# Loads of the experts' rows for the first two token tiles: from one issuing queue to three

## The chip, the cores and the metric

The kernel runs on one core of one Trainium2 chip. A core has engines that work side by side, each on its own instruction stream: TensorE (PE, with its weight loads shown as PEld), VectorE (DVE), ScalarE (ACT), GpSimd (POOL) and SyncE (SP). SP, ACT and POOL can also issue transfers (DMAs) between device memory and the on-chip memory; 16 DMA engines carry them. The metric is device time in microseconds (us), the median of three executions.

## The reference

Two decoder layers over 512 tokens of width 1024. What matters here is the second half of a layer: a mixture of 16 experts, of which every token takes two, and a gated residual behind it.

```python
y = jnp.zeros(x.shape, jnp.float32)
for e in range(N_EXPERTS):
    hdn = jax.nn.silu(x @ w_gate[e]) * (x @ w_up[e])
    y = y + combine[..., e:e + 1] * (hdn @ w_down[e])       # combine: two weights a token
...
h = h + hier_moe(rmsnorm(h, ffn_norm[i]), ...)
gate = jax.nn.sigmoid(rmsnorm(h, ple_norm[i]) @ ple_gate_w[i] + ple_gate_b[i])
h = h + gate * (p[i] @ ple_proj[i])
```

## The kernel before

The 512 tokens are four tiles `h[0]` to `h[3]` of 128 tokens by 1024 columns, kept in on-chip memory. For every expert the kernel gathers up to 128 tokens' rows, multiplies them, and POOL scatters the resulting rows (`ys`) to a table `yd` in device memory (line 1203). The table has 2 x 512 rows: for each token one row from its first expert (k = 0) and one from its second (k = 1).

A loop for overflowing experts follows (`overflow`, line 1251), whose count is a value computed on the chip. Here it runs no pass, but every engine goes through its entry and its end, and there waits until the others have come to it and the scatters have landed.

Then comes `combine`. For tile i and expert rank k it loads 128 rows of `yd` into a tile `yt[i, k]` (line 1363): tile 0 in two column halves of 512 (256 KB each), the other tiles whole (512 KB each). That makes ten loads a layer, in the order of tiles. The words `COMB` (lines 63 to 68), one string for each layer, give the order of the steps behind it. Each step puts its instructions at the end of its engines' streams, so no engine runs ahead of that order in its own stream:

- `p3`: three pieces of the embedding's projection (PE line 1347, copied out by ACT line 1348).
- `c000`, `c010`, `c011`, `c001`: add a half of `yt` times the token's weight to `h[0]` (DVE line 1372). The digits are tile, rank k, half; `c10`, `c11` and so on add a whole tile.
- `t00`, `t01`: PE transposes a half of `h[0]` (line 251); ACT makes its rounded high part `n3h` (line 221), and DVE the low part `n3l` (line 222). `t1` to `t3` do both halves of a tile.
- `g00` and so on: the gate's matmuls (lines 255 to 257, three for each product); `n0` and so on: the squared sum and the reciprocal root of a row's norm (ACT line 210, POOL lines 204 and 205).

The first layer begins `p3 c000 c010 t00 c011 c001 p2 n0 p1 t01 c11 c10 g00 t1`, the second `p3 c000 c010 t00 c001 c011 p1 p2 c11 t01 n0 c10 p3 p9 n1 c20`.

Between the loop and `c000` one more piece of the gate's weights is prepared: ACT makes two 128x512 high parts `wh` (line 232), DVE two low parts `wl` (line 243). They stand ahead of `c000` in DVE's stream. Behind the ten loads SP's stream has the rest of the gate's weights (`wr<-wpg`, line 114) and the next layer's first ones (`wr<-win`).

Of the kernel before, what the change touches and what calls it, by code (L numbers as in the profile page):

```python
# [23 lines left out]
S = 512  # L24
# [143 lines left out]
class _Kernel:  # L168
# [1160 lines left out]
    def combine(self):  # L1329
        nc, V, T, SC, w, h, l, tk = self.nc, self.V, self.T, self.SC, self.w, self.h, self.l, self.ticks  # L1330
# [25 lines left out]
        yt = {}  # L1356
# [3 lines left out]
        for i in range(NT):  # L1360
            for ns in (slice(0, 512), slice(512, D)) if not i else (slice(0, D),):
                for k in range(2):
                    nc.sync.dma_start(yt[i, k][:, ns], self.yd[k * S + i * 128:k * S + (i + 1) * 128, ns])
        w.limit = 10 ** 9
        rn, xn, n3, o, gt, ss = {}, {}, {}, {}, {}, {}

# [210 lines left out]
```

## Time and profile before

| | |
|---|---|
| median of three runs | 925.35 us (923.51 to 927.01) |
| the profiled execution | 925.41 us, its span 923.6 us |
| granted TensorE clock, mean | 0.973 |
| busy share of the span | PE 93%, DVE 77%, ACT 56%, POOL 16% |
| the ten loads of a layer, issued by SP | first layer 399.50 to 406.85 us, second 852.08 to 857.63 us |

A time in a row counts from the start of the span. PE is nearly always busy, so a change in these stretches counts as far as it moves PE's next work: between the loop and the gate's first matmul PE has idle gaps, and each is put down to what ended it. "issue" means that the engine waited for nothing that the profile shows, which here is the way out of the loop.

### The profile page before, as it was taken

To read this page: it belongs to the slowest core of one execution; us is meant where nothing else is said; L and a number is where in the kernel's file an instruction comes from. 1 tells how busy PE (TensorE), PEld (TensorE's weight loads), DVE (VectorE), ACT (ScalarE), POOL (GpSimd) and SP (SyncE) were. 2 spreads that over 40 slices of the span, in tenths; PEclk is the share of its full clock that TensorE was granted. 3 is DMA by queue.
4 is the path that set the end of the run, shared out by engine and by line. 5 is a ranking of instruction groups with operands and counts; after the bars stand their busy time and mean duration, and the time that the engine had idled before them with its cause. 6 is when DMAs were issued, how large, how long until landed. Compare 5 with 4: busy or idle time off the path is not lost. (4 is left out here: it accounts for less than half of the span.)

```text
span 923.6 us, 12348 instructions
## 1 busy us (share of the span) xinstructions
PE 858.0 (93%) x4393; PEld 687.6 (74%) x4393; DVE 715.4 (77%) x1182; ACT 519.1 (56%) x945; POOL 151.2 (16%) x214
## 2 busy tenths in 40 slices
PE   7999988897999999979979999989979999998994
PEld 5888876685677777767878887767847777776783
DVE  4599989966788888746676998998478888885674
ACT  4322246853687878745433233487347778776453
POOL 2040001122222211101010300022131222111101
PEclk9999999998999999999999999989979999999998
DMA  9222230158799979563322223110958998882602
GB/s 354 106 92 96 98 114 1 46 193 309 270 347 363 370 271 340 227 234 146 114 92 92 92 103 112 49 46 24 373 216 307 359 370 324 317 321 91 260 24 91
DMA packets 35775, 179.02 MB, mean 194 GB/s; under 512 B 8064, under 2 KB 8320, under 8 KB 18944
## 3 DMA queue, kind: packets, MB, share of 16 engines
q1 hardware_dynamic: 23472, 148.49, 43.1%
q0 software_dynamic: 9792, 20.99, 6.2%
q10 hardware_dynamic: 2448, 8.73, 2.6%
q8 instruction: 35, 0.57, 0.2%
q14 instruction: 28, 0.23, 0.1%
HBM read 171.89 MB, written 23.07 MB: 211 GB/s over the span
## 5 line engine op out<-in xcount | busy, mean ns | idle before, releaser
L239 DVE TENSOR_TENSOR wl<-wr,wh 128x1024 fp32r<-128x1024 f32 x212 | 253.1, 1220 | 41.4 <-ACT wh L228 40.1
L228 ACT CAST wh<-wr 128x1024 fp32r<-128x1024 f32 x212 | 216.2, 1053 | 91.1 <-PE mm L256 60.9
L255 PE MATMUL mm<-wh,xTh 128*128 128x512 f32 x256 | 113.9, 445 | 1.0 <-ACT xTh L221 1.0
L483 DVE SCALAR_TENSOR_TENSOR acc<-glu,cwh,acc 128x512 f32<-128x512 f32 x120 | 100.5, 837 | 3.4
L257 PE MATMUL mm<-wh,xTl 128*128 128x512 f32 x256 | 101.2, 395 | 1.2 <-DVE xTl L222 1.2
L256 PE MATMUL mm<-wl,xTh 128*128 128x512 f32 x256 | 100.5, 392 | 0.0
L257 PE MATMUL mm<-nhi,wl 128*128 128x512 f32 (+1 forms) x224 | 77.3, 345 | 2.5 <-DVE wl L239 2.5
L255 PE MATMUL mm<-nhi,wh 128*128 128x512 f32 (+1 forms) x224 | 77.1, 344 | 0.0
L256 PE MATMUL mm<-nlo,wh 128*128 128x512 f32 (+1 forms) x224 | 77.0, 344 | 0.0
L255 PEld LDWEIGHTS mm<-wh,xTh 128*128 128x128 f32 x256 | 48.1, 188 | 16.9 <-issue 6.7
L1241 PE MATMUL mm<-wr,hT 128*128 128x512 f32 x128 | 60.2, 592 | 0.0
L1198 POOL DMA_INDIRECT xg<-xnd,ix x32 | 35.4, 1105 | 149.8 <-PE tr L251 136.8
L256 PEld LDWEIGHTS mm<-wl,xTh 128*128 128x128 f32 x256 | 48.2, 188 | 15.3 <-DVE wl L239 6.2
L257 PEld LDWEIGHTS mm<-wh,xTl 128*128 128x128 f32 x256 | 48.0, 188 | 12.9 <-DVE xTl L222 2.9
L255 PE MATMUL mm<-wh,mhi 128*128 128x512 f32 x128 | 54.0, 422 | 1.0 <-DVE h L750 1.0
L1203 POOL DMA_INDIRECT yd<-ys,ix x32 | 32.3, 1010 | 122.9 <-ACT ys L1243 107.3
L255 PE MATMUL mm<-wh,n3h 128*128 128x512 f32 x128 | 50.6, 395 | 0.0
L257 PE MATMUL mm<-wh,mlo 128*128 128x512 f32 x128 | 50.3, 393 | 0.0
L256 PE MATMUL mm<-wl,mhi 128*128 128x512 f32 x128 | 50.0, 391 | 0.0
L257 PE MATMUL mm<-wh,n3l 128*128 128x512 f32 x128 | 49.9, 390 | 0.0
L256 PE MATMUL mm<-wl,n3h 128*128 128x512 f32 x128 | 49.9, 390 | 0.0
L257 PEld LDWEIGHTS mm<-nhi,wl 128*128 128x128 f32 x224 | 42.4, 189 | 8.2 <-DVE wl L239 3.2
(236 smaller groups left out, 1861.6 us busy)
## 6 DMA issues: line engine op xcount, KB each, us to landing
wr<-wgu SPq DMA_DIRECT2D x62, 1024.0 KB, 9.1
wr<-wdn SPq DMA_DIRECT2D x30, 1024.0 KB, 10.8
wr<-win SPq DMA_DIRECT2D x13, 1024.0 KB, 6.2
wr<-wout SPq DMA_DIRECT2D x8, 1024.0 KB, 4.8
wr<-wpg SPq DMA_DIRECT2D x8, 1024.0 KB, 13.8
yt<-yd SPq DMA_DIRECT2D x12, 512.0 KB, 8.1
wr<-wqk SPq DMA_DIRECT2D x4, 1024.0 KB, 4.8
xnd<-xn ACTq DMA_DIRECT2D x8, 512.0 KB, 4.0
```

The costliest lines, as they stand in the source:

```text
L228: self.SC.copy(hi, src)
L239: self.V.tensor_sub(lo, src, h32)
L255: self.T.matmul(o, lh, rh, start=first, stop=False)
L256: self.T.matmul(o, lh, rl, start=False, stop=False)
L257: self.T.matmul(o, ll, rh, start=False, stop=last)
L483: V.scalar_tensor_tensor(acc[:, m], glu[:, m, k:k + S], self.cwh[:, m, k:k + 1], acc[:, m], op0=ALU.mult, op1=ALU.add)
L1198: return self.G.indirect_dma_start(out=dst, out_offset=None, in_=self.xnd[:, :], in_offset=bass.IndirectOffsetOnAxis(ap=col, axis=0), boun ...
L1203: return self.G.indirect_dma_start(out=self.yd[:, :], out_offset=bass.IndirectOffsetOnAxis(ap=col, axis=0), in_=src, in_offset=None, bound ...
L1241: self.T.matmul(o[nh], hT[:, c], wc[:, ns], start=(c == 0), stop=(c == 1))
```

## The change

The loads for rank k = 1 of the first two token tiles are issued by other engines: the two halves of tile 0 (`yt[0, 1]`) by ACT, the whole of tile 1 (`yt[1, 1]`) by POOL. The other loads stay on SP, in the same order. Lines of the changed kernel behind this one have a number higher by one.

```diff
         for i in range(NT):
             for ns in (slice(0, 512), slice(512, D)) if not i else (slice(0, D),):
                 for k in range(2):
-                    nc.sync.dma_start(yt[i, k][:, ns], self.yd[k * S + i * 128:k * S + (i + 1) * 128, ns])
+                    q = (SC, self.G)[i] if k and i < 2 else nc.sync
+                    q.dma_start(yt[i, k][:, ns], self.yd[k * S + i * 128:k * S + (i + 1) * 128, ns])
```

SP's stream in the first layer, behind the loop's end; `yt01` is tile 0 rank 1, `yt11` tile 1 rank 1. Before:

```order
L1363 DMA yt00_4153<-yd0_2304 128x512
L1363 DMA yt01_4154<-yd0_2304 128x512
L1363 DMA yt00_4153<-yd0_2304 128x512
L1363 DMA yt01_4154<-yd0_2304 128x512
L1363 DMA yt10_4155<-yd0_2304 128x1024
L1363 DMA yt11_4156<-yd0_2304 128x1024
L1363 DMA yt20_4157<-yd0_2304 128x1024
```

And now:

```order
L1364 DMA yt00_4153<-yd0_2304 128x512 x2
L1364 DMA yt10_4155<-yd0_2304 128x1024
L1364 DMA yt20_4157<-yd0_2304 128x1024
L1364 DMA yt21_4158<-yd0_2304 128x1024
L1364 DMA yt30_4159<-yd0_2304 128x1024
L1364 DMA yt31_4160<-yd0_2304 128x1024
L114 DMA wr_4171<-wpg 128x2048
```

SP has seven issues where it had ten, and the second half of `yt00` is now its second load. ACT's stream in the first layer, at the same place, the changed kernel against the one before:

```order
 L1251 COMPARE_AND_BRANCH
 L1251 UNCONDITIONAL_BRANCH
+L1364 DMA yt_4154<-yd_2304 128x512 x2
 L232 ACTIVATE wh<-wr,pgain 128x512 x2
 L1348 ACTIVATE pp_3987<-mm 128x256
```

Both issues stand ahead of the two `wh` of the gate's weights. On POOL the load of `yt11` stands between the loop's end and the first norm's `r` (line 204).

## Rows read from the trace of the kernel before

**Rows 1.** Waits, 390 to 430 us: who <- whom: us in total, times, longest.
```profile
POOL r L204 <- DMA yt<-yd: 16.6, 1, 16.6
...
PE tr L251 <- DVE h L1372: 4.5, 3, 1.6
...
DVE h L1372 <- DMA yt<-yd: 1.8, 2, 1.1
```

**Rows 2.** Waits, 845 to 880 us.
```profile
PE tr L251 <- DVE h L1372: 0.3, 1, 0.3
```

**Rows 3.** Timeline of DVE, first layer: start, us, what [idle before <- releaser].
```profile
401.39 1.41 DVE L243 SCALAR_TENSOR_TENSOR wl<-wr,pgain,wh 128x512 fp32r<-128x512 f32 x2 [6.18 <-ACT wh L232]
...
404.23 0.75 DVE L1372 SCALAR_TENSOR_TENSOR h<-yt,wts,h 128x512 f32<-128x512 f32 x1 [0.67 <-DMA yt<-yd]
406.35 0.69 DVE L222 TENSOR_TENSOR n3l<-tr,n3h 128x512 fp32r<-128x512 f32 x1 [1.37 <-ACT n3h L221]
408.16 1.54 DVE L1372 SCALAR_TENSOR_TENSOR h<-yt,wts,h 128x512 f32<-128x512 f32 x2 [1.12 <-DMA yt<-yd]
```

**Rows 4.** Timeline of PE, first layer.
```profile
405.04 0.66 PE L251 MATMUL tr<-con,h 128*128 128x128 f32 x4 [1.46 <-DVE h L1372]
405.53 2.75 PE L1347 MATMUL mm<-wr,pT 128*128 128x256 f32 x12
409.75 0.44 PE L251 MATMUL tr<-con,h 128*128 128x128 f32 x2 [1.47 <-DVE h L1372]
```

**Rows 5.** Timeline of SP, loads one by one: three of the first layer, one of the second.
```profile
399.50 0.33 SPq L1363 DMA_DIRECT2D yt<-yd  x1
...
399.87 1.79 SPq L1363 DMA_DIRECT2D yt<-yd  x1
...
402.38 0.42 SPq L1363 DMA_DIRECT2D yt<-yd  x1
...
852.08 0.33 SPq L1363 DMA_DIRECT2D yt<-yd  x1
```

**Rows 6.** Landing times: loads 2 and 4 (first layer), 2 (second): us from issue.
```profile
yt<-yd SPq DMA_DIRECT2D x1, 256.0 KB, 4.3
...
yt<-yd SPq DMA_DIRECT2D x1, 256.0 KB, 5.7
...
yt<-yd SPq DMA_DIRECT2D x1, 256.0 KB, 3.8
```

**Rows 7.** Stretches, first layer: busy us by engine, PEclk, DMA share, GB/s.
```profile
401.20:402.40 1.20, 1.20 (x7) 1.04 (x7) 1.01 (x2) 1.07 (x3) 0.00 (x0) 1.00 0.25 63
...
408.20:414.00 5.80, 4.33 (x22) 3.60 (x22) 3.76 (x5) 1.90 (x4) 0.76 (x2) 1.00 1.03 420
```

**Rows 8.** Timeline of ACT, its first instructions behind the loop, both layers.
```profile
400.63 1.33 ACT L232 ACTIVATE wh<-wr,pgain 128x512 fp32r<-128x512 f32 x2 [1.65 <-issue]
...
853.20 1.33 ACT L232 ACTIVATE wh<-wr,pgain 128x512 fp32r<-128x512 f32 x2 [1.46 <-issue]
```

**Rows 9.** By tile and line: DMA issues of ACT (gv) and POOL (wgu), ns min/median/max.
```profile
L200 ACTq DMA_DIRECT2D gv<-gv x6: 334/340/378, 121.2 to 882.3; - x6
...
L114 POOL DMA_DIRECT2D wr<-wgu x2: 614/616/617, 233.3 to 685.3; - x2
...
DMA to landing us min/median/max: 5.8/7.0/8.1
```

**Rows 10.** Timeline of DVE and PE, second layer.
```profile
856.31 0.75 DVE L1372 SCALAR_TENSOR_TENSOR h<-yt,wts,h 128x512 f32<-128x512 f32 x1 [0.28 <-DMA yt<-yd]
...
859.54 2.84 DVE L1372 SCALAR_TENSOR_TENSOR h<-yt,wts,h 128x512 f32<-128x512 f32 x3
...
853.30 4.54 PE L1347 MATMUL mm<-wr,pT 128*128 128x256 f32 x12 [1.98 <-issue]
857.68 0.60 PE L251 MATMUL tr<-con,h 128*128 128x128 f32 x4
```

**Rows 11.** Stretches, second layer: the projection's matmuls behind the loop.
```profile
853.44:856.86 3.42, 3.42 (x9) 2.71 (x10) 2.63 (x4) 1.48 (x3) 0.00 (x0) 0.50 1.05 284
```

## The prediction

> **What bounds the kernel now.** I first read the waits of the two stretches that the change touches, since the loads are used only between the overflow loop and the gate. In the first layer DVE's `c` steps wait 1.8 us in two pieces for loads of `yt`, and PE's transposes wait 4.5 us in three pieces for those steps; POOL waits 16.6 us and has nothing else to do [rows 1]. In the second layer PE waits for them once, 0.3 us [rows 2]. So there is some 3 us to win in the first layer at most, and next to nothing in the second.
>
> Then the timelines, in the order of the chain. First layer: SP issues load 2 (`yt01`, half 0) at 399.87 [rows 5]; it lands after 4.3 us [rows 6], at 404.2, and `c010` starts at 404.23 after an idle 0.67 [rows 3]. It ends at 404.98, and `t00` starts at 405.04 [rows 4]. DVE's `n3l` for it ends at 406.35 + 0.69 = 407.04, 2.00 behind the start of `t00`. Then DVE is idle for 1.12 until load 4 (`yt01`, half 1) has landed: issued at 402.38, 5.7 us, so 408.1. `c011` and `c001` take 1.54 from 408.16 to 409.70, and `t01` starts at 409.75. PE had idled 1.47 there; its projections had ended at 405.53 + 2.75 = 408.28 [rows 3 to 6]. Load 4 is late because SP's issue of load 2 took 1.79 where others take 0.33 and 0.42 [rows 5]: from 401.20 to 402.40 the DMA engines were busy for 0.25 of the time, and later, with all loads queued, for all of it at 420 GB/s [rows 7].
>
> Second layer: no such stall. `c010` waits 0.28 for its load, but `t00` starts at 857.68 because PE's twelve projections end there: they take 4.54 [rows 10], at a granted clock of 0.50 from 853.44 to 856.86 [rows 11], against 2.75 for the same twelve in the first layer [rows 4]. `c001`, `c011` and `c11` then run without a gap, 2.84 for the three [rows 10]; their data was there.
>
> **The change part by part.** *Three loads leave SP.* This saves SP three issues of about 0.42 [rows 5]. Nothing waits for SP's later loads in these stretches, so in itself it is worth 0. What can be worth something is the hole of 401.20 to 402.40 [rows 7], which other queues may fill. In the second layer there is no wait of PE that an earlier load could end, so 0 there.
>
> The Trainium skill ("DMA: Bandwidth & Descriptors", Issuing engines are not separate DMA queues) says that DMAs from several engines run on the same 16 DMA engines, and that issuing from several saves only the issuing time. The rows agree where the DMA engines are full, at 420 GB/s, and not in the hole, where the issue itself was what was late. By the rule alone the sum would be the 0 of the paragraph above.
>
> *Two issues enter ACT's stream, ahead of `wh`.* ACT's own issues cost 0.34 each [rows 9], so 0.68; the bounds are 0.66, two of SP's cheapest, and 3.6, two of its 1.79 [rows 5]. I take 0.68, from ACT's rows. First layer: `wl` ends at 401.39 + 1.41 + 0.68 = 403.48, `c000` 0.75 later, and `c010` could start at 404.23, just when it does now: its old wait of 0.67 hides the two issues. Without that cover they would cost 0.68. Second layer: `c010` could start at 856.31 - 0.28 + 0.68 = 856.71 [rows 10]; it needs to end by about 857.62 for `t00` at 857.68, so to start by 856.87. Hidden, with 0.16 to spare.
>
> *`yt01` is issued later, by ACT.* ACT does its first work behind the loop at 400.63 and 853.20 [rows 8], SP at 399.50 and 852.08 [rows 5]: ACT is out 1.1 us later, and that is 0.76 behind load 2's old issue in the first layer (399.87) and about 0.7 in the second (856.31 less 3.8 is 852.5). When it lands is the unknown. The nearest rows are the same load's 4.3 (first layer) and 3.8 (second); the upper end is load 4's 5.7 [rows 6]; the lower end is that it is no longer late at all. In the first layer I take 4.3: landed at 404.93, `c010` 0.70 later than now, `t00` at 405.74, its `n3l` done at 407.74. Half 1, issued at 400.97 with 4.3 to 5.7, lands at 405.3 to 406.7, and `yt00`'s half 1, now SP's second load, at 399.87 + 4.3 = 404.2 or 405.6 with 5.7. Both are there before 407.74, so DVE's wait of 1.12 is gone: 407.74 + 1.54 + 0.05 puts `t01` at 409.33, not 409.75. Gain 0.42. The ends: with no load late, `t00` stays at 405.04 and `t01` comes at 405.04 + 2.00 + 1.54 + 0.05 = 408.63, a gain of 1.12 (PE is free at 408.28). With 5.7 `c010` starts at 406.33, 2.10 late, and `t01` at 410.73, a loss of 0.98. The break-even is `c010` at 405.35.
>
> In the second layer 3.8 gives 857.0, `c010` done at 857.75, `t00` at 857.81: a loss of 0.13. With 4.3 it is 0.63, with 5.7 it is 2.03, with no lateness 0. Since `yt11` is now in flight beside it, I take the middle of the two near rows, 0.38.
>
> *`yt11` moves to POOL.* An issue costs POOL 0.61 [rows 9], hidden in its wait of 16.6 [rows 1]; without that cover, 0.61. POOL's loads landed after 5.8 to 8.1 us at twice the size [rows 9], so by 408.3 in the first layer, if POOL leaves the loop when SP does, and 860.8 in the second. It is used by `c11`: in the first layer behind the `n3l` of `t01` (which starts at 409.75); in the second after `c001` and `c011`, at 859.54 + 1.5 = 861.0. So 0, with bounds of 0 below and, for a landing 1 us later than any of these, 0.8 in the second layer.
>
> *Sum:* -0.42 + 0.38 = -0.04. The gate's matmuls follow `t01` on PE, so what `t00` and `t01` move, moves the rest. From the profiled execution's 925.41, which stands 0.06 above the median of 925.35: **925.3 us**, no change. The ends add up to -1.1 and +3.0 (and 0.8 for POOL).
>
> **The rivals.**
> - *The hole fills and nothing is late.* For it: 0.25 busy in that hole [rows 7], where ACT's and POOL's loads would now be queued. Against: ACT is out 1.1 later. Gain 1.12 in the first layer, 0 in the second: 924.2.
> - *Slower: the first-needed load takes turns.* In one queue `yt01` stood ahead of `yt10` and `yt11`; in three it shares the DMA engines with them while it is still short of data. It then needs load 4's 5.7, which was also served among others. Price 0.98 + 2.03 = 3.0: 928.4. It decides from a `c010` later than 405.35 in the first layer and than 856.87 in the second. For it: both starts are near (404.93, 857.0). Against: loads 2 and 4 landed in 3.8 to 5.7 although other loads stood ahead of them in their one queue [rows 6]. The Trainium skill (same page, Queues, rings and completion order) says that each DMA engine goes round robin between the queues that have work, packet by packet. No row of this kernel shows three queues at once; by that rule this rival would hold as far as POOL's packets are ahead of ACT's.
> - *The clock.* Behind the loop PE had idled 1.98 when it ran at 0.50 in the second layer; the same twelve projections cost 1.79 more there [rows 4, 10, 11]. If a later `t00` brings that to the first layer too: 927.2. If the second layer's stretch falls elsewhere, it can as well be 923.6.
>
> **How the numbers follow.** Chances: forecast 0.55, hole filled 0.17, turns 0.18, clock 0.10. A measurement of this kernel can tell about 0.5%, that is 4.6 us, from no change: below 920.7 or above 930.0. For slower by that, turns and clock must come together (3.0 + 1.8 = 4.8): 0.04. For faster, the hole's 1.1 and the clock's 1.8 don't do: 0.03 for what I haven't seen. Same: 0.93. The three runs shown spread from 923.5 to 927.0 by themselves; with the cases' ends of 924.2 and 928.4, and about one in ten left out on each side, the range is 922.9 to 928.3.
>
> **What would show it.** In the profile after: ACT issues two loads near 400.6 and 853.2, at 0.34 each; `c010` starts near 404.9 and 857.0; DVE's wait of 1.12 before `c011` is gone; `t01` of the first layer near 409.3, `t00` of the second within 0.6 of 857.7 (if the way there takes as long). It is wrong if ACT's issues take over 1 us each, so that `wh` becomes what `c000` waits for; if POOL's load makes `c11` wait; or if the stall of 1.79 comes from something that the new streams shift elsewhere.

## The result and the profile after

The changed kernel takes 936.27 us (median of six runs, 932.49 to 941.43), the kernel before 925.51 in the same six rounds. The ratio is 1.0123, its 95% interval 1.0098 to 1.0148: slower by 1.2%, some 11 us, where no change was forecast and 928.3 was the upper end of the range.

The profiled execution is the slowest of the six (941.43 us, span 939.7, granted clock 0.963). By SP's first load of the first layer it is already 4.95 us behind the profile of before (404.45 to 399.50, [rows 5]), and nothing in the program differs up to there; the granted clock up to that point was 0.96 against 0.98. So the stretches are compared from SP's first load on. The waits of the second layer, after, 853 to 890 us (who <- whom: us in total, times, longest):

```profile
PEld tr L251 <- DVE h L1373: 6.4, 1, 6.4
DVE h L1373 <- DMA yt<-yd: 5.9, 1, 5.9
PE tr L251 <- DVE h L1373: 5.7, 1, 5.7
```

Here PE waited 0.3 us before [rows 2]. In the first layer it is 4.9 where it was 4.5 [rows 1], but in other places: 3.4 of it ahead of `t00`, and none ahead of `t01`. The chain that ended last now has the loads in it, which it had not before (shares of the span by engine, from the page):

```profile
PE 6%; DMA 1%; DVE 0%; ACT 0%; issue 0%; POOL 0%; POOLq 0%; ACTq 0%; DVEq 0%
```

DVE after, first layer and then second (start, us, what [idle before <- releaser]), to be held against [rows 3, 10]:

```profile
408.53 0.75 DVE L1373 SCALAR_TENSOR_TENSOR h<-yt,wts,h 128x512 f32<-128x512 f32 x1
411.08 0.75 DVE L1373 SCALAR_TENSOR_TENSOR h<-yt,wts,h 128x512 f32<-128x512 f32 x1 [1.81 <-DMA yt<-yd]
413.60 0.69 DVE L222 TENSOR_TENSOR n3l<-tr,n3h 128x512 fp32r<-128x512 f32 x1 [1.76 <-ACT n3h L221]
414.20 1.53 DVE L1373 SCALAR_TENSOR_TENSOR h<-yt,wts,h 128x512 f32<-128x512 f32 x2
...
864.45 0.75 DVE L1373 SCALAR_TENSOR_TENSOR h<-yt,wts,h 128x512 f32<-128x512 f32 x1
871.10 0.75 DVE L1373 SCALAR_TENSOR_TENSOR h<-yt,wts,h 128x512 f32<-128x512 f32 x1 [5.90 <-DMA yt<-yd]
874.28 2.73 DVE L1373 SCALAR_TENSOR_TENSOR h<-yt,wts,h 128x512 f32<-128x512 f32 x3
```

`c010` waits 1.81 and 5.90 us for its load, where it waited 0.67 and 0.28. The old wait of 1.12 ahead of `c011` is gone, as forecast. PE of the same two stretches, to be held against [rows 4, 10]:

```profile
411.89 1.05 PE L251 MATMUL tr<-con,h 128*128 128x128 f32 x4 [3.35 <-DVE h L1373]
412.74 4.08 PE L1347 MATMUL mm<-wr,pT 128*128 128x256 f32 x12
416.65 0.60 PE L251 MATMUL tr<-con,h 128*128 128x128 f32 x4
...
871.90 1.11 PE L251 MATMUL tr<-con,h 128*128 128x128 f32 x4 [5.74 <-DVE h L1373]
872.81 4.44 PE L1347 MATMUL mm<-wr,pT 128*128 128x256 f32 x12
```

`t00` of the second layer comes 871.90 - 860.40 = 11.5 us behind SP's first load, where it came 5.6 behind (857.68 - 852.08). Then the twelve projections take 4.44, not 2.76: PE had idled 5.74, and the clock is at its lower level (0.50). The same twelve before:

```profile
858.12 2.76 PE L1347 MATMUL mm<-wr,pT 128*128 128x256 f32 x12
```

Two stretches of the second layer after, with columns as in [rows 7]; the first is the wait, the second reaches from `t00` to the first gate matmul:

```profile
867.00:869.50 2.50, 0.00 (x0) 0.00 (x0) 0.00 (x0) 0.00 (x0) 0.00 (x0) 0.98 0.99 361
...
871.90:879.90 8.00, 8.00 (x31) 6.85 (x32) 4.86 (x6) 3.91 (x9) 0.44 (x1) 0.73 0.87 362
```

In the first of them no compute engine does anything, and the DMA engines are as good as full (0.99, 361 GB/s): they are carrying mostly other loads (0.56 MB of SP's queue, 0.06 of POOL's, 0.28 of ACT's). ACT's loads were issued in time and cheaply, and landed late (issue of the second layer's two; then their landing times in us, first layer 5.4 and 6.9, second 9.5 and 11.0):

```profile
861.50 0.34 ACTq L1364 DMA_DIRECT2D yt<-yd  x1
...
861.87 0.45 ACTq L1364 DMA_DIRECT2D yt<-yd  x1
```

```profile
yt<-yd ACTq DMA_DIRECT2D x1, 256.0 KB, 5.4
...
yt<-yd ACTq DMA_DIRECT2D x1, 256.0 KB, 6.9
...
yt<-yd ACTq DMA_DIRECT2D x1, 256.0 KB, 9.5
...
yt<-yd ACTq DMA_DIRECT2D x1, 256.0 KB, 11.0
```

From SP's first load to the first gate matmul, the kernel before takes 10.7 and 11.9 us in the two layers, the changed one 12.6 and 19.5. That is 1.9 + 7.6 = 9.5 us more in one execution, against 10.8 between the medians. The clock has a part in the first layer too: PE had idled 3.35 ahead of `t00`, and the twelve projections behind it then took 4.08 where they had taken 2.75 [rows 4], with the clock at 0.50 for most of them (stretch of the first layer after):

```profile
412.00:415.41 3.41, 3.41 (x11) 2.87 (x12) 1.78 (x3) 0.97 (x2) 0.00 (x0) 0.50 1.03 415
```

### The profile page after: what moved, and what is told of

It reads as the page before. It is cut to its first block, busy times and chain, and to the rows that moved or that the text cites. A ratio compares the mean times of both kernels' runs of the same rounds, so it can differ in the third digit from the quotient of the medians.

```text
span 939.7 us, 12350 instructions
## 1 busy us (share of the span) xinstructions
PE 864.7 (92%) x4393; PEld 694.0 (74%) x4393; DVE 715.8 (76%) x1182; ACT 518.7 (55%) x945; POOL 150.5 (16%) x216
## 5 line engine op out<-in xcount | busy, mean ns | idle before, releaser
L221 ACT CAST xTh<-tr 128x512 fp32r<-128x512 f32 x64 | 34.5, 589 | 25.7 <-PE tr L251 24.1
```

What stands on the lines that cost most here:

```text
L221: self.SC.copy(hi, src)
```

## The experiments

Each kernel has another owner, or another moment, for the loads; merged has other loads, and after_warm more matmuls. "Gate" is the time from SP's first load to the first gate matmul, in the first and the second layer, read from each kernel's timeline. Ratios are to the kernel before, in rounds on the same chip; they are estimates over all runs, and need not be the quotient of two medians. A gate is from one execution: the change's is its slowest of six, act_hold's its fastest of ten. A gate also includes what the clock does behind a late `t00`: from `t00` to the gate it takes 3.9 us in the first layer and 6.4 in the second with the clock at 1.00 (act_hold), and 5.1 and 8.0 in the change.

| kernel | loads off SP | ratio (95%) | gate, us |
|---|---|---|---|
| before | none | 1 | 10.7 / 11.9 |
| the change | yt01 ACT, yt11 POOL | 1.0123 (1.0098 to 1.0148) | 12.6 / 19.5 |
| act_only | yt01 ACT | 1.0071 (1.0049 to 1.0093) | 11.5 / 16.8 |
| pool_only | yt11 POOL | 1.0023 (1.0002 to 1.0045) | 12.1 / 13.7 |
| all_act | yt01, yt11 ACT | 1.0077 (1.0050 to 1.0105) | 10.2 / 16.0 |
| late_tiles | yt21 ACT, yt31 POOL | 1.0093 (1.0058 to 1.0128) | 15.0 / 17.3 |
| act_hold | yt01 ACT, rest of SP held | 0.9999 (0.9982 to 1.0017) | 9.8 / 12.0 |
| three_hold | as the change, rest of SP held | 1.0093 (1.0062 to 1.0123) | 11.9 / 17.6 |
| all_hold | as the change, POOL and rest of SP held | 1.0016 (1.0000 to 1.0033) | 9.6 / 12.0 |
| pool_hold | yt11 POOL, rest of SP held | 1.0072 (1.0049 to 1.0096) | 12.4 / 13.6 |
| after_warm | as the change | 1.0087 (1.0060 to 1.0113) | (below) |
| merged | none, five loads a layer | 1.0027 (1.0008 to 1.0046) | 9.5 / 12.9 |

**Which part of the change: act_only, pool_only, all_act.** Each with one line:

```diff
-                    q = (SC, self.G)[i] if k and i < 2 else nc.sync
+                    q = SC if k and i == 0 else nc.sync        # act_only
+                    q = self.G if k and i == 1 else nc.sync    # pool_only
+                    q = SC if k and i < 2 else nc.sync         # all_act
```

> Only the two halves of yt01 go to ACT; yt11 stays on SP. Theory A (POOL's load is the cause: it puts tile 1's 512 KB ahead of tile 0 and slows ACT's loads): about as the kernel before, 924 to 928 us, and c010 in the second layer waits under 1 us for its load. Theory B (ACT's loads are the cause: they come 1.1 us after SP's and then take turns with SP's whole backlog): nearly all of the loss stays, 932 to 937 us, with c010 in the second layer waiting 3 to 6 us.

> Only yt11 goes to POOL; yt01 stays on SP between the two halves of yt00. Theory A: most of the loss stays, 931 to 937 us, and the four halves land over 2 us later than in the kernel before. Theory B: 924 to 928 us; the halves land at most 1.5 us later, since POOL's 512 KB share the DMA engines with them, and c11 does not wait.

> yt01 (two halves) and yt11 all on ACT, none on POOL: two hardware queues. Theory A: 924 to 928 us. Theory B: 932 to 938 us, c010 as late as with three queues, since ACT's first load still stands against SP's backlog.

Measured: 932.49, 928.61 and 932.45 us. Theory B holds for the larger part: act_only keeps 0.71 of the change's 1.23%. It does not hold for all of it. pool_only is slower too (1.0023, its interval just clear of 1), and in its second layer the two loads of half 1 land 4.5 and 3.5 us later than in the kernel before, not 1.5 at most. The two parts add up to 0.94%, which the intervals don't tell from 1.23. In all_act's first layer `c010` does not wait at all (gate 10.2), so "as late as with three queues" fails there. In act_only's second layer `c010` waits 3.09, and `yt01`'s first half lands 6.7 after its issue, as does the 512 KB load of `yt10` that SP had issued just ahead of it:

```profile
860.94 0.75 DVE L1373 SCALAR_TENSOR_TENSOR h<-yt,wts,h 128x512 f32<-128x512 f32 x1 [3.09 <-DMA yt<-yd]
```

```profile
yt<-yd SPq DMA_DIRECT2D x1, 512.0 KB, 6.7
...
yt<-yd ACTq DMA_DIRECT2D x1, 256.0 KB, 6.7
```

**Is it what the moved loads are needed for: late_tiles.**

```diff
-                    q = (SC, self.G)[i] if k and i < 2 else nc.sync
+                    q = (SC, self.G)[i - 2] if k and i >= 2 else nc.sync
```

> Three queues as in the change, but with the loads that are needed last: yt21 on ACT, yt31 on POOL; tiles 0 and 1 stay on SP in their old order. If three queues at once are slow whatever they carry: 930 to 937 us. If only what the loads are needed for counts (theory B): 924 to 928 us, since c20 to c31 come over 8 us after the loop and tile 0 is ahead in SP's queue. Theory A: 930 us or more, since POOL's load again takes turns with tile 0.

Measured 937.24 us: theory B as put there falls. Tile 0 stands in SP's queue as it always did, ACT and POOL carry loads that nobody needs for ten microseconds, and tile 0 is late all the same. DVE, the first layer's `c010` and the second layer's `c001`:

```profile
411.16 0.75 DVE L1373 SCALAR_TENSOR_TENSOR h<-yt,wts,h 128x512 f32<-128x512 f32 x1 [3.57 <-DMA yt<-yd]
...
869.56 1.54 DVE L1373 SCALAR_TENSOR_TENSOR h<-yt,wts,h 128x512 f32<-128x512 f32 x2 [3.60 <-DMA yt<-yd]
```

The median lies just above what "slow whatever they carry" had (930 to 937). So it is not that ACT comes out of the loop late, nor that its loads are the ones waited for. What tile 0 loses is its place: in one queue it stands ahead of everything else.

**Tile 0 alone, or with company: act_hold, three_hold, all_hold, pool_hold.** A copy of one column from `yt01` into `yt10`, on the idle POOL, makes SP wait with `yt10` and all behind it until `yt01`'s first half has landed; the load then overwrites that column.

```diff
         for i in range(NT):
+            if i == 1:
+                self.G.tensor_copy(yt[1, 0][:, 0:1], yt[0, 1][:, 0:1])
```

In act_hold and all_hold the copy stands there, so that in all_hold POOL's own load waits as well; in three_hold and pool_hold, where the loop is written out as a list, POOL issues `yt11` ahead of the copy.

> yt01 on ACT as in act_only, and SP's loads of tiles 1 to 3 held back: a copy of one column on POOL, from yt01's first half into yt10, lets SP go on when that half has landed (the load then overwrites the column). Theory C (turns: the loads of a later tile that are queued on another queue are served beside tile 0's, so tile 0 lands with them): with nothing queued beside them yt01's halves land within 5 us of their issue in both layers (7.8 and more in act_only), c010 in the second layer waits under 1.5 us, total 924 to 928 us. Theory D (ACT's queue is slow by itself, or what costs is the 1.1 us that ACT is out of the loop later): c010 still waits about 3 us in the second layer, total 930 to 934 us.

> The change with the same hold for SP's loads of yt10 and of tiles 2 and 3: only POOL's 512 KB of yt11 are served beside tile 0. Theory C: between act_hold and the change, 926 to 931 us, with yt01's halves landing 1 to 3 us later than in act_hold. If SP's backlog has no part in it: 934 to 938 us, as the change.

> The change's three queues, but both POOL's load of yt11 and SP's loads of yt10 and tiles 2 and 3 wait (through the one-column copy on POOL) until yt01's first half has landed; tile 0 is alone on SP and ACT. Theory C (only what is served beside tile 0 costs): yt01 lands within 5 us of its issue, c010 waits under 1.5 us, the first gate as in act_hold; c11 may wait 1 to 4 us in the second layer since POOL's load starts late: 925 to 930 us. Theory E (a load on POOL's queue costs by being there at all): 932 us or more.

> All of tile 0 on SP, yt11 on POOL at once, SP's other loads held until yt01's first half has landed; ACT issues none. If POOL's load is slow on a few DMA engines and whatever is queued on another queue is served there one for one with it: SP's second half of yt00 and the halves of yt01 again land near POOL's load in the second layer (7 to 9 us behind the first issue, 4.1 to 6.1 in the kernel before), total 927 to 932 us. If POOL's load only delays ACT's loads: 924 to 927 us, tile 0 landed within 6.5 us.

Measured 926.57, 935.57, 926.45 and 931.29 us. act_hold and act_only have the same loads on the same queues and differ only in whether SP's later loads are in flight beside `yt01`: 0.9999 (0.9982 to 1.0017) against 1.0071 (1.0049 to 1.0093). three_hold and all_hold differ only in whether POOL's load is: 1.0093 against 1.0016, the intervals apart as well. Theory D (ACT's queue slow by itself) and theory E (POOL's queue costs by being there) fall. DVE in the second layer, act_hold first (`c000` and `c010` in a row, no wait between them) and then three_hold (`c010` after 4.52 of waiting):

```profile
854.92 1.54 DVE L1375 SCALAR_TENSOR_TENSOR h<-yt,wts,h 128x512 f32<-128x512 f32 x2
```

```profile
863.55 0.75 DVE L1375 SCALAR_TENSOR_TENSOR h<-yt,wts,h 128x512 f32<-128x512 f32 x1 [4.52 <-DMA yt<-yd]
```

Theory C's number for three_hold failed: 926 to 931 us were expected, and 935.57 lies where "SP's backlog has no part in it" was put (934 to 938). The change is not told from three_hold either (1.0123 and 1.0093, the intervals overlap): holding SP's backlog back brings little as long as POOL's load is in flight. That the backlog has no part is not so, since act_only loses 0.7% to it against act_hold without any load on POOL. Either company alone costs more than half of what both cost together.

three_hold also shows that POOL's load is more than 512 KB of company. In the second layer it and tile 0's 1 MB are all there is to carry (but for one fetch of 16 KB), and yet it lands after 8.5 us and ACT's two after 8.1 and 8.2; in the first layer it is 5.3, and 4.9 and 6.0. In that time the DMA engines are first full and then nearly idle (stretches of the second layer, columns as before, DMA share and GB/s last):

```profile
858.20:860.20 2.00, 0.10 (x1) 0.00 (x0) 0.82 (x2) 0.38 (x1) 0.00 (x0) 1.00 0.97 326
860.20:862.20 2.00, 0.00 (x0) 0.00 (x0) 0.00 (x0) 0.00 (x0) 0.00 (x0) 0.65 0.26 95
862.20:863.90 1.70, 0.00 (x0) 0.00 (x0) 0.35 (x1) 0.00 (x0) 0.18 (x1) 0.50 0.05 19
```

A load counts as landed when all 16 of its parts are, and the trace has the time of each. In us from SP's first load of the second layer, from the events of the loads' semaphores:

```
before      yt01 half 0 (SP)     2.8 2.8 2.9 3.0 3.1 3.2 3.2 3.2 3.4 3.5 3.5 3.5 3.6 3.7 4.0 4.1
three_hold  yt11 (POOL)          4.7 4.9 4.9 5.0 5.1 5.1 5.2 5.5 5.5 5.6 5.6 6.5 7.4 7.4 7.4 9.0
three_hold  yt01 half 0 (ACT)    5.4 5.6 5.6 5.6 5.7 5.7 5.8 5.8 5.8 5.8 6.2 6.7 7.6 7.6 7.6 9.2
act_hold    yt01 half 0 (ACT)    3.6 3.6 3.6 3.6 3.7 3.7 3.7 3.8 3.9 3.9 4.0 4.2 4.3 4.3 4.5 4.7
```

Put in order of landing, ACT's parts follow POOL's at 0.2 to 0.7 us, the last four included, with the same steps between them. A load waits for the slowest of its 16 parts. The trace does not say which DMA engine a part is from; that ACT's last four are from the engines of POOL's last four is likely by these times, and not shown.

In pool_hold all of tile 0 is on SP, with POOL's load as its only company, and it is slower than before all the same (1.0072). Its time is also above pool_only's (1.0023, the intervals just apart), although the gate of the two profiles is nearly the same (12.4 / 13.6 and 12.1 / 13.7). These profiles can't show the difference, since the executions took nearly the same time: 931.69 us, and for pool_only 932.30, the slowest of its ten. Where it lies stays open.

**The clock: after_warm.** 24 matmuls on constants (`w24` in the second layer's order) where PE idled.

```diff
-        "p3 c000 c010 t00 c001 c011 ...
+        "p3 w24 c000 c010 t00 c001 c011 ...
...
+            "w": lambda a, b: self.warm(10 * a + b),
```

> The change with 24 more matmuls on constants (results unused) in the second layer, between the projections and t00, where PE idled 5.7 us and then ran at the lower clock. If the lower clock behind the wait is part of the loss: 1.5 to 2.5 us faster than the change, 933.5 to 935 us, and the granted clock at t00 is 1.00. If the clock has no part: 936 us or more.

Measured 933.85 us, 2.4 below the change's median; the two ratios' intervals overlap (1.0087 and 1.0123), so the profile must carry it. There the clock is 1.00 from `t00` on, and from `t00` to the first gate matmul it takes 6.35 us (863.93 to 870.28) where the change took 8.03 (871.90 to 879.93):

```profile
863.90:870.30 6.40, 6.14 (x34) 5.17 (x32) 4.91 (x6) 3.92 (x9) 0.49 (x1) 1.00 1.03 430
```

So the lower clock behind the wait is worth 1.7 us there. The first layer of after_warm has the same instructions as the change, and its `t00` comes as late, 7.46 us behind SP's first load (7.44 in the change). But its stretch at the lower clock fell earlier, on the projections ahead of `t00`, behind which PE had to wait anyway; from `t00` on the clock was 1.00, and its gate comes at 11.4, not 12.6. PE and the stretch from `t00` to the gate, first layer of after_warm:

```profile
408.06 0.66 PE L251 MATMUL tr<-con,h 128*128 128x128 f32 x4 [1.77 <-DVE h L1373]
408.55 2.76 PE L1347 MATMUL mm<-wr,pT 128*128 128x256 f32 x12
```

```profile
408.06:411.98 3.92, 3.66 (x21) 3.01 (x21) 2.10 (x3) 1.79 (x4) 0.00 (x0) 1.00 1.03 417
```

By this comparison 1.2 of the change's 1.9 us in the first layer are the clock's, in the execution that was profiled, and 0.7 the late loads'.

**Fewer issues instead of more queues: merged.**

```diff
+        both = self.yd[:, :].rearrange("(k s) d -> s k d", k=2)
...
+            yi = yp.tile([128, 2, D], F32, name=f"yt{i}")
...
-                for k in range(2):
-                    nc.sync.dma_start(yt[i, k][:, ns], ...)
+                nc.sync.dma_start(yi[:, :, ns], both[i * 128:(i + 1) * 128, :, ns])
```

> The kernel before with one load for both ranks (tile 0 in two halves of 512 KB, tiles 1 to 3 of 1 MB each), all on SP: five issues a layer and not ten, one queue. In the first layer tile 0's second half should land 1 to 2 us earlier than in the kernel before (8.6 us behind the first issue), so t01 comes up to 1.1 us earlier; the second layer as before. 924 to 926 us, not to be told from the kernel before by its time alone.

Measured 928.84 us, above the range, and 1.0027 (1.0008 to 1.0046): slower by 0.3%. The first layer's gate comes 1.2 us earlier, as expected; in the second layer `c000` now waits 1.61 for both ranks, and the gate comes 0.9 later. No kernel here beats the one before; act_hold can't be told from it.

## Why the prediction was wrong, point by point

- *Where to look* was right: 9.5 us of the profiled execution's loss, against 10.8 between the medians, lie between the loop and the gate.
- *Two issues on ACT, 0.68, hidden*: right. They took 0.34 and 0.45, and `c000` at 4.1 us behind SP's first load was not what anything waited for.
- *`yt01` issued later, its landing taken from 4.3 and 3.8, the upper end 5.7*: this is the step that failed, as a size, and in the second layer above all. It measured 5.4 (first layer, within the bounds) and 9.5 (second) from the issue. `c010` started 6.6 and 10.7 us behind SP's first load, where the forecast had 5.4 and 4.9 (404.93 - 399.50, 857.0 - 852.08). The term for the second layer was 0.38 with an end of 2.03; `t00` came 5.9 us later. In the first layer a gain of 0.42 was forecast, with an end of -0.98; the gate came 1.9 later, 0.7 of it without the clock (after_warm). The bound was taken from loads of one queue [rows 6]. Such a row tells how long a load waits behind what stands ahead of it. It does not tell how long it takes when what stands *behind* it in the order of need is served beside it.
- *`yt00` half 1, now SP's second load, there by 405.6*: wrong in the first layer, 6.8 us behind the first load where 6.1 was the end. It too had company (alone with ACT's two loads, in all_hold, it landed at 5.4). The long issue of SP's second load, 1.79 before, is still there too: 1.36, now on this load.
- *`yt11` on POOL, 0*: right for its user (`c11` does not wait) and wrong for its neighbours: no cost to them was entered, and three_hold against all_hold puts it at 0.8% (pool_only, with nothing on ACT, at 0.2%). The row for POOL's loads, 5.8 to 8.1 [rows 9], would have been a better upper end for whatever is served with them, though 9.5 lies beyond it too.
- *The rival "the first-needed load takes turns"* named the mechanism, with 0.18 and a price of 3.0. act_hold against act_only shows it for SP's backlog, all_hold against three_hold for POOL's load, and late_tiles that tile 0 is late on its old queue too. It was priced by the same 5.7. By the Trainium skill ("DMA: Bandwidth & Descriptors", Queues, rings and completion order) each DMA engine takes the queues that have work in turn. The runs agree: `yt01`'s first half landed 9.5 us after its issue with the other queues at work, and 3.6 in act_hold. The Trainium skill also says (same page, Issuing engines are not separate DMA queues) that issuing from several engines saves only the issuing time. By that alone the sum would have been 0; the measured +1.2% shows that it can cost, through the order.
- *The clock rival* came on top, at 1.7 us in the second layer and, in the profiled execution, 1.2 in the first, where the rival had put it (1.8). Both times it stood behind a long wait of PE (5.74 and 3.35). The prediction had said that a slowdown clear of the noise needs turns and clock together, with a chance of 0.04; both came, and the turns cost about twice their price of 3.0 (0.7 + 5.9 = 6.6).
- *The hole that other queues may fill* was there to fill, and the old wait ahead of `c011` went. all_hold's and act_hold's first layer (gate at 9.6 and 9.8, 10.7 before) show that gain of about 1 us, once tile 0 is alone. Their times don't show it (0.9999 and 1.0016).

Open: why POOL's load costs so much more in the second layer than in the first (it lands after 8.7 and 5.7 us in the change; in all_hold, issued behind tile 0, after 5.2 and 5.1), and why a few parts lag by 2 to 4 us.

## What to carry to other kernels

One queue is also an order: whatever stands in it ahead is served first (the ten loads of the kernel before land in their order, from 3.0 to 14.0 us behind the first issue in the second layer). Before moving a load to a second queue, ask what will be in flight beside it, and bound its landing by the landing of that, not by its own size. If more queues are wanted, hold back the loads that are not needed yet; here the hold took the loss away (0.9999 with ACT's loads, 1.0016 with three queues) and won nothing.

## What the runs showed of the hardware

A 512 KB load issued by POOL took 8.5 us with 1 MB beside it, while the DMA engines were idle for much of the last 3 us (0.26, then 0.05 busy): 12 of its 16 parts had landed 2.5 us ahead of the last. In order of landing, the parts of ACT's load beside it lagged in the same steps, and its 16 parts landed over 3.8 us. In the kernel before, with one queue, the 16 parts of each 256 KB load land within 1.0 to 1.7 us in the second layer, and within 0.7 to 2.8 in the first.

The long issue on which the prediction built (1.79) goes with a fetch of instructions. In ten of the twelve traces a 16 KB fetch starts 0.3 to 0.4 us behind SP's first load of the first layer; SP's second issue then takes 1.3 to 1.8 us and ends 0.37 to 0.39 after the fetch. In the other two, act_only and act_hold, the fetch starts at 0.9, and SP's second issue takes 0.42. No run took the fetch away.
